# First layer's FFN shift and gate on VectorE, one unbroken norm-factor run, final products on two engines

## The chip, the cores and the metric

The kernel runs on one core of one Trainium2 chip. The metric is device time in microseconds (us) for one execution, as the median of several runs; lower is better. An execution holds a span, which the profile cuts into its engines' work, and a little time around it.

## The reference

Two layers of a diffusion backbone work on 384 token columns: 128 context tokens and 256 latent tokens. Each layer has six modulation vectors of 1024 channels, one column of each for the context tokens and one for the latent tokens. They come from one matrix product of a conditioning vector with `w_ada`:

```
mod = silu(c) @ w_ada[l] + b_ada[l]          # shift1, scale1, gate1, shift2, scale2, gate2
h = rms_norm(x) * (1 + scale1) + shift1
out = mix(h)                                  # three token mixers, gated, one output projection
x = x + gate1 * out
h = rms_norm(x) * (1 + scale2) + shift2
a, b = split(h @ w_ffn_in)
x = x + gate2 * ((silu(a) * b) @ w_ffn_out)
```

After both layers the output is `rms_norm(x, final_norm)`: x times one factor per token and one gain per channel.

## The kernel before

Activations are held transposed: 128 channels on the partitions, eight channel tiles, 384 tokens in the free direction. Every dense product is made in three matmuls of split operands: a weight piece of 128x1024 is loaded as `raw`, ScalarE rounds it to `wh`, and VectorE (for the FFN's second half every other time GpSimd) subtracts to get `wl` (`piece`, L659). One output tile of `dense_t` (L686) is 24 matmuls of 384 columns into a PSUM buffer `d`, of which there are three. `raw` has four buffers, `wh` and `wl` three each.

The weight pieces are read in one fixed order that `stream` (L64) writes down; the entries of other kinds that stand between them (`gate`, `ada`, `adv`) are worked off on the way by `piece`. All instructions are first recorded and then put in order by a planner (`Recorder.order`, L383): a list schedule with costs per instruction and an urgency per recorded operation, in which each engine takes the most urgent operation that is ready. Engines then run their instructions in that fixed order. One recorded operation is normally one instruction; one with several calls is never interleaved with others.

The parts around the change:

- **Modulation vectors of layer 0.** The first two are made at the start (`ada`, L753). The other four come in two groups of eight steps, spread over the 24 tiles of the first layer's branch projections. A step (`ada_step`, L791) loads two `raw` pieces and issues four fp32 matmuls of 512 columns on 32-column tiles (tile `m<-raw,silc`); after eight steps two ScalarE copies, four transposes (`m<-cst,sc`) and one addition of the bias follow. The places are ordered (L58-59), so that group 1 is gate1 and scale2, and group 2 is shift2 and gate2.
- **Modulation vectors of layer 1.** These are made on VectorE during the first layer's FFN (`ada_block`, L818): 48 blocks, each one `raw` piece and two VectorE instructions of 128x1024 that multiply it with one of two broadcast rows (tile `PL`) and sum it into one column of `mod`.
- **Norm factor.** `ssq` (L871) squares a channel tile on ScalarE and adds it into `nacc`; the eighth square isn't added. Matmuls with ones sum `nacc` and the eighth square over the partitions, three each (`m<-ones,nacc`, `m<-ones,sc`). `ssq_end` (L885) copies one result with ScalarE, adds the other, runs twelve small VectorE instructions on 128x3 (`rsqrt`, L739), makes three diagonal tiles and broadcasts them by one matmul. `norm_end` (L898) copies that to SBUF as `nacc` (named `rb` in the code). There are seven such norms: at the start, and in each layer after the SSD mixer, after the output projection and after the FFN. FFN tiles leave PSUM through a multiplication with `rb` (`sc<-d,nacc`), so the first of them waits for it.
- **Final norm.** Eight VectorE instructions multiply x by the gain and by the factor in PSUM (`PH<-PH,cst,m`), each followed by the DMA of its tile from SyncE.

## Time and profile before

| what | us |
|---|---|
| runs, median of 3 (lowest, highest) | 1911.48 (1909.68, 1913.89) |
| the profiled execution | 1913.74 |
| its span | 1912.0 |
| TensorE (PE) busy | 1864.8 |
| VectorE (DVE) busy | 1373.3 |
| ScalarE (ACT) busy | 944.3 |
| GpSimd (POOL) busy | 362.2 |

The profile's rows name an engine, an operation and the tiles it writes and reads. PE is the matmul part of TensorE, PEld its weight loads, which overlap the matmuls, and SPq the DMA queue of SyncE. Nearly all rows carry the line of the place that issues recorded operations (L516), so that the tile names tell them apart. A number in square brackets behind a row is the idle time of the engine before it, with what ended it.

### The profile page before, as it was taken

The page shows a single profiled execution, that of the slowest core. Times are in us where ns is not written, and L with a number is a line of the kernel's source. Part 1 is how long each engine was busy: PE and PEld are TensorE (multiplying, and loading weights), DVE is VectorE, ACT ScalarE, POOL GpSimd, SP SyncE. Part 2 cuts the span into 40 slices and gives each one's busy share as a digit, 9 for nine tenths or more (in the row PEclk, how much of TensorE's full clock was granted, in tenths as well). Part 3 has the DMA queues.
Part 4 walks back from the last instruction along what each step waited for, and adds up shares of the span by engine and source line. Part 5 has one row for each costly group of instructions (what it writes and reads, how often), then busy time and mean ns, then how long its engine had stood idle before and what let it go on. Part 6 is the DMA issues. An engine that isn't in the chain of part 4 may idle for free. (4 is left out here: it accounts for less than half of the span.)

```text
span 1912.0 us, 30336 instructions
## 1 busy us (share of the span) xinstructions
PE 1864.8 (98%) x10998; PEld 1726.6 (90%) x10998; DVE 1373.3 (72%) x2923; ACT 944.3 (49%) x1905; POOL 362.2 (19%) x362
## 2 busy tenths in 40 slices
PE   6999999999999999999999999999999999999997
PEld 5998998788988889999999889987879999999997
DVE  5847876888845598998978588768987567666522
ACT  4545555666522344443446556556755434444431
POOL 0112421230101111113511224112300022000132
PEclk9999999999999999999999999999999999999998
DMA  8566344664578766666654664346544554443341
GB/s 312 141 171 206 124 125 132 161 168 124 162 261 275 234 203 187 217 207 216 213 202 132 170 188 128 122 141 168 157 119 142 167 165 156 124 127 124 122 123 65
DMA packets 119318, 319.38 MB, mean 167 GB/s; under 512 B 13952, under 2 KB 57344, under 8 KB 117504
## 3 DMA queue, kind: packets, MB, share of 16 engines
q1 hardware_dynamic: 119168, 317.44, 54.3%
q8 instruction: 87, 1.43, 0.3%
q14 instruction: 63, 0.52, 0.1%
HBM read 296.59 MB, written 19.75 MB: 165 GB/s over the span
## 5 line engine op out<-in xcount | busy, mean ns | idle before, releaser
L516 ACT ACTIVATE wh<-raw 128x1024 fp32r<-128x1024 f32 x374 | 395.8, 1059 | 564.8 <-PE d L516 524.1
L516 DVE TENSOR_TENSOR wl<-raw,wh 128x1024 fp32r<-128x1024 f32 x352 | 454.9, 1293 | 226.3 <-ACT wh L516 223.6
L516 PE MATMUL d<-HH,wh 128*128 128x384 f32 x1448 | 496.5, 350 | 0.0
L516 PE MATMUL d<-HL,wh 128*128 128x384 f32 x1416 | 469.3, 337 | 0.0
L516 PE MATMUL d<-HH,wl 128*128 128x384 f32 x1384 | 466.5, 337 | 0.0
L516 PEld LDWEIGHTS d<-HH,wh 128*128 128x128 f32 x1448 | 273.1, 189 | 21.8 <-issue 15.9
L516 PEld LDWEIGHTS d<-HL,wh 128*128 128x128 f32 x1416 | 267.2, 189 | 0.6
L516 PEld LDWEIGHTS d<-HH,wl 128*128 128x128 f32 x1384 | 261.2, 189 | 0.0
L516 PE MATMUL d<-A,wh 128*128 128x386 f32 x744 | 255.4, 343 | 4.3 <-DVE sc L516 4.1
L516 PE MATMUL d<-C,wh 128*128 128x386 f32 x744 | 252.8, 340 | 0.0
L516 PE MATMUL d<-A,wl 128*128 128x386 f32 x744 | 252.8, 340 | 0.0
L516 PEld LDWEIGHTS d<-A,wh 128*128 128x128 f32 x744 | 140.9, 189 | 5.3 <-issue 4.4
L516 PEld LDWEIGHTS d<-C,wh 128*128 128x128 f32 x744 | 141.8, 191 | 0.4
L516 PEld LDWEIGHTS d<-A,wl 128*128 128x128 f32 x744 | 140.6, 189 | 0.0
L516 POOL TENSOR_TENSOR sc<-sc,sc 128x126 f32<-128x126 f32 x112 | 61.7, 569 | 272.4 <-DVE sc L516 159.7
L516 DVE SCALAR_TENSOR_TENSOR PH<-PL,n,cst 128x128 f32<-128x128 f32 x288 | 100.2, 381 | 14.6 <-PE l L516 5.3
L516 POOL TENSOR_TENSOR wl<-raw,wh 128x1024 fp32r<-128x1024 f32 x22 | 56.6, 2571 | 269.2 <-ACT sh L516 193.1
L516 PE MATMUL d<-wh,HH 128*128 128x512 f32 x240 | 98.1, 409 | 0.0
L516 PE MATMUL d<-wh,HL 128*128 128x512 f32 x240 | 95.0, 396 | 0.0
L516 PE MATMUL d<-wl,HH 128*128 128x512 f32 x240 | 95.0, 396 | 0.0
L516 PE MATMUL d<-PH,wh 128*128 128x384 f32 x256 | 87.2, 340 | 0.0
L516 PE MATMUL d<-PH,wl 128*128 128x384 f32 x256 | 86.1, 336 | 0.0
(260 smaller groups left out, 3130.3 us busy)
## 6 DMA issues: line engine op xcount, KB each, us to landing
raw<-in_ws SPq DMA_DIRECT2D x454, 512.0 KB, 3.7
PL<-rowr SPq DMA_DIRECT2D x48, 384.0 KB, 5.6
gd<-sc SPq DMA_DIRECT2D x48, 192.0 KB, 1.9
pb<-gd SPq DMA_DIRECT2D x48, 192.0 KB, 2.8
ex<-rowe SPq DMA_DIRECT2D x32, 128.0 KB, 3.7
ex<-rowe SPq DMA_DIRECT2D x16, 256.0 KB, 5.9
PH<-in_xT SPq DMA_DIRECT2D x2, 1536.0 KB, 7.4
yad<-pb SPq DMA_DIRECT2D x16, 192.0 KB, 1.9
```

Of the source, the lines that this page charges most:

```text
L516: tc.keep_in_program_order(getattr(engines[op.eng], meth)(*[real(a) for a in args], **{k: real(v) for k, v in kw.items()}))
```

## The change

- The eight steps of group 2 leave the stream. In their place 16 blocks of `ada_block`, for shift2 and gate2 of layer 0, stand around the eight steps of group 1. The broadcast rows for them lie in tile `F`. The number of weight pieces stays the same.
- The layer-1 blocks begin behind the fifth FFN piece of layer 0 instead of the first: 30 blocks now stand in 39 pieces of the first half and 18 in the second half, where 32 in 44 and 16 stood.
- `ssq` adds the eighth square too, on VectorE, and sums with three matmuls. `ssq_end` records the twelve small instructions, which now read PSUM directly, and the three diagonal tiles as one operation (`together`).
- In the last FFN ScalarE multiplies x by the final gain. At the end ScalarE copies the factor to SBUF, GpSimd multiplies tiles 0 and 1 by the copy, and VectorE the other six by the factor in PSUM.

```diff
+ADV_FROM = 5
...
-        s += main if l else main[:at] + spread(main[at:], steps(0, 1, 2))
+        late = []
+        for i, it in enumerate(steps(0, 1)):
+            late += [(("adv", 0, SHIFT2, i), 1), it, (("adv", 0, GATE2, i), 1)]
+        s += main if l else main[:at] + spread(main[at:], late)
...
-            at = len(blocks) * len(ff) // len(ff + fo)
-            s += spread(ff, blocks[:at]) + spread(fo, blocks[at:])
+            n = len(ff) - ADV_FROM
+            at = len(blocks) * n // (n + len(fo))
+            s += ff[:ADV_FROM] + spread(ff[ADV_FROM:], blocks[:at]) + spread(fo, blocks[at:])
...
+    @contextmanager
+    def together(self):
+        nc, calls = self.nc, []
+        class Collect:
+            def __getattr__(self, meth):
+                return lambda *a, **k: calls.append((meth, a, k))
+        old, nc.vector = nc.vector, Collect()
+        yield
+        nc.vector = old
+        op = self.rec.rec("vector", calls)
+        op.cost = max(op.cost, 0.196 * len(calls))
...
-        if self.spos == self.adv_at:
-            t = self.slot("PL", [P, 3, D])
+        if self.silb is None or self.silb[0] != l:
+            t = self.slot("PL" if l else "F", [P, 3, D])
...
-        elif j < KT - 1:
-            add(self.nacc, self.nacc, sq, ALU.add)
-        else:
+            return
+        (add if j < KT - 1 else self.tt)(self.nacc, self.nacc, sq, ALU.add)
+        if j == KT - 1:
             self.nps = self.mps()
-            for i, v in enumerate((self.nacc, sq)):
-                for t in range(3):
-                    self.mm(self.nps[:, 3 * i + t:3 * i + t + 1], v[:, t * P:t * P + P], self.ones[:, 0:1])
+            for t in range(3):
+                self.mm(self.nps[:, t:t + 1], self.nacc[:, t * P:t * P + P], self.ones[:, 0:1])
...
-        s = self.ring("r3", [P, 3])
-        self.act(s, self.nps[:, 0:3], AF.Copy)
-        self.tt(s, s, self.nps[:, 3:6], ALU.add)
-        self.rsqrt(r, s, 1.0 / n, eps, [P, 3])
         dg = self.sc()
-        for t in range(3):
-            self.ts(dg[:, t * P:t * P + P], self.ident, r[:, t:t + 1], ALU.mult)
+        with self.together():
+            self.rsqrt(r, self.nps[:, 0:3], 1.0 / n, eps, [P, 3])
+            for t in range(3):
+                self.ts(dg[:, t * P:t * P + P], self.ident, r[:, t:t + 1], ALU.mult)
...
                 if l + 1 < LAYERS:
                     self.scaled(l + 1, SHIFT1, SCALE1, j)
+                else:
+                    self.act(self.x[:, j], self.x[:, j], AF.Copy, scale=self.cst("fin")[:, j:j + 1])
...
-        for j in range(8):
-            self.stt(self.x[:, j], self.x[:, j], fin[:, j:j + 1], rb, ALU.mult, ALU.mult)
+        rs = self.sc()
+        self.act(rs, rb, AF.Copy)
+        for j in (0, 2, 3, 4, 5, 1, 6, 7):
+            if j < 2:
+                self.ptt(self.x[:, j], self.x[:, j], rs, ALU.mult)
+            else:
+                self.tt(self.x[:, j], self.x[:, j], rb, ALU.mult)
             self.dma(self.O["yT"][:, j], self.x[:, j])
```

How the order of instructions moves, at the three places that the prediction speaks of. Numbers behind a name tell buffers apart; PL with `mod_14` are the blocks of layer 1, F with `mod_13` those of layer 0, C the operand of the FFN, `rs` and `r` the norm factor.

VectorE at the step from the first layer's output projection to its FFN, before:

```order
L516 TENSOR_TENSOR r_1317_7330<-r_1317_7330,m_7318 128x3
L516 SCALAR_TENSOR_TENSOR C_7021<-PH_6953,mod_13_250,A_7013 128x128
L516 TENSOR_SCALAR rs_7342<-r_1317_7330 128x3
L516 SCALAR_TENSOR_TENSOR C_7021<-PH_6953,mod_13_250,A_7013 128x256
L516 TENSOR_SCALAR rs_7348<-rs_7342 128x3
L516 SCALAR_TENSOR_TENSOR PL_6956,mod_14_7104<-raw_7305,PL_6956 128x1024
L516 TENSOR_SCALAR rs_7348<-rs_7348 128x3
L516 SCALAR_TENSOR_TENSOR C_7021<-PH_6953,mod_13_250,A_7013 128x128
L516 SCALAR_TENSOR_TENSOR rs_7363<-rs_7348 128x3
L516 SCALAR_TENSOR_TENSOR raw_7305,mod_14_7104<-raw_7305,PL_6956 128x1024
```

The same place in the change:

```order
L523 TENSOR_TENSOR nacc_7002<-nacc_7002,sc_7269 128x384
L523 SCALAR_TENSOR_TENSOR PL_6939,mod_14_7284<-raw_7239,PL_6939 128x1024
L523 SCALAR_TENSOR_TENSOR C_7004<-PH_6936,mod_13_241,A_6996 128x128
L523 TENSOR_SCALAR rs_7294<-m_7286 128x3
L523 TENSOR_SCALAR rs_7296<-rs_7294 128x3
L523 TENSOR_SCALAR rs_7296<-rs_7296 128x3
L523 SCALAR_TENSOR_TENSOR rs_7299<-rs_7296 128x3
L523 TENSOR_TENSOR rs_7299<-rs_7299,rs_7294 128x3
```

The small instructions of the norm factor stood between blocks of layer 1 and now follow each other; one half of a block stands ahead of them.

VectorE in the first layer's branch projections, before:

```order
L516 SCALAR_TENSOR_TENSOR E_5996<-pb_5010,d_5990 128x384
L516 TENSOR_TENSOR wl_6053<-raw_5970,wh_6042 128x1024
L516 SCALAR_TENSOR_TENSOR E_5996<-pb_5033,d_6038 128x384
L516 TENSOR_TENSOR wl_6095<-raw_6011,wh_6084 128x1024
L516 SCALAR_TENSOR_TENSOR E_5996<-pb_5177,d_6080 128x384
```

The same place in the change:

```order
L523 SCALAR_TENSOR_TENSOR raw_5839,mod_13_241<-raw_5839,F_5306 128x1024
L523 SCALAR_TENSOR_TENSOR F_5306,mod_13_241<-raw_5862,F_5306 128x1024
L523 SCALAR_TENSOR_TENSOR C_2295<-sc_5893,C_2295 128x384
L523 SCALAR_TENSOR_TENSOR raw_5862,mod_13_241<-raw_5862,F_5306 128x1024
L523 TENSOR_TENSOR wl_5947<-raw_5843,wh_5925 128x1024
L523 TENSOR_TENSOR HL_5959<-C_2295,HH_5937 128x384 x3
L523 SCALAR_TENSOR_TENSOR E_5979<-pb_4832,d_5921 128x384
```

Between one weight tile `wl` and the next there now stand up to two blocks of two instructions each.

VectorE at the end of the program, before, with what an instruction waits for in brackets (PE_49, DVE_49 and Activation_49 are the counters of TensorE, VectorE and ScalarE):

```order
L516 SCALAR_TENSOR_TENSOR r_3372_19251<-rs_19242,rs_19239 128x3 [waits DVE_49]
L516 TENSOR_SCALAR sc_19253<-cst_97,r_3372_19251 128x128 [waits DVE_49]
L516 TENSOR_SCALAR sc_19253<-cst_97,r_3372_19251 128x128 x2
L516 SCALAR_TENSOR_TENSOR PH_16440<-PH_16440,cst_97,m_19257 128x384 [waits PE_49]
L516 SCALAR_TENSOR_TENSOR PH_16440<-PH_16440,cst_97,m_19257 128x384 x7
```

The same place in the change:

```order
L523 SCALAR_TENSOR_TENSOR r_3363_19217<-rs_19208,rs_19205 128x3 [waits DVE_49]
L523 TENSOR_SCALAR sc_19219<-cst_97,r_3363_19217 128x128 [waits DVE_49]
L523 TENSOR_SCALAR sc_19219<-cst_97,r_3363_19217 128x128 x2
L523 TENSOR_TENSOR PH_16408<-PH_16408,m_19223 128x384 [waits Activation_49]
L523 TENSOR_TENSOR PH_16408<-PH_16408,m_19223 128x384 x5
```

VectorE's first product waited for the broadcast matmul and now waits for ScalarE, whose last instruction is the copy of the same PSUM tile.

## Rows read from the trace of the kernel before

**Rows 1.** The page: busy time, share of the span and instructions of each engine.

```profile
PE 1864.8 (98%) x10998; PEld 1726.6 (90%) x10998; DVE 1373.3 (72%) x2923; ACT 944.3 (49%) x1905; POOL 362.2 (19%) x362
```

**Rows 2.** Stretches (us): length, busy time by engine, granted clock, DMA share, GB/s.

```profile
521.00:660.00 139.00, 137.44 (x792) 116.70 (x792) 70.38 (x92) 41.94 (x60) 19.20 (x21) 1.00 0.76 251
750.00:850.00 100.00, 100.00 (x566) 100.00 (x565) 94.98 (x153) 46.80 (x95) 16.53 (x12) 1.00 0.65 211
```

**Rows 3.** Timeline of PE around one step of the modulation matmuls: start, length, instruction.

```profile
521.18 0.34 PE L516 MATMUL d<-HL,wh 128*128 128x384 f32 x1
521.35 0.34 PE L516 MATMUL d<-HH,wl 128*128 128x384 f32 x1
521.62 1.07 PE L516 MATMUL m<-raw,silc 128*32 128x512 f32 x8
...
522.90 0.33 PE L516 MATMUL d<-HL,wh 128*128 128x384 f32 x1
```

**Rows 4.** Groups on PE, 521 to 660 us: busy, mean ns | idle before.

```profile
L516 PE MATMUL m<-raw,silc 128*32 128x512 f32 x128 | 20.7, 605 | 1.6 <-DMA raw<-in_ws 1.4
L516 PE MATMUL m<-cst,sc 128*128 128x128 f32 x8 | 1.3, 287 | 0.0
```

**Rows 5.** Waits, 521 to 660 us: total us, times, longest.

```profile
PEld m L516 <- DMA raw<-in_ws: 5.2, 6, 1.3
```

**Rows 6.** Timeline of PE: second half of one norm's sums, and the next matmul.

```profile
505.14 0.81 PE L516 MATMUL m<-ones,sc 128*128 128x1 f32 x6
505.81 0.42 PE L516 MATMUL d<-HH,wh 128*128 128x384 f32 x1
```

**Rows 7.** Timeline of PE at the first layer's step into its FFN.

```profile
708.71 0.34 PE L516 MATMUL d<-A,wl 128*128 128x386 f32 x1
713.17 0.41 PE L516 MATMUL d<-A,wh 128*128 128x386 f32 x1 [4.12 <-DVE sc L516]
...
717.81 0.34 PE L516 MATMUL d<-A,wl 128*128 128x386 f32 x1
```

**Rows 8.** The same place: timeline of DVE.

```profile
700.18 0.14 DVE L516 TENSOR_TENSOR r<-r,m 128x3 f32<-128x3 f32 x1
...
705.65 0.68 DVE L516 TENSOR_SCALAR sc<-cst,r 128x128 f32<-128x128 f32 x3
...
712.47 1.48 DVE L516 TENSOR_TENSOR sc<-d,nacc 128x384 f32<-128x384 f32 x3
```

**Rows 9.** The same place: ACT copies the factor out of PSUM.

```profile
708.09 0.49 ACT L516 ACTIVATE nacc<-m 128x384 f32<-128x384 f32 x1 [0.29 <-PE m L516]
```

**Rows 10.** The same place as a stretch, columns as in rows 2.

```profile
710.00:720.00 10.00, 6.83 (x30) 6.86 (x31) 9.27 (x17) 4.03 (x9) 1.38 (x1) 0.83 0.56 196
```

**Rows 11.** Groups on DVE, 750 to 850 us: the two instructions of a layer-1 block.

```profile
L516 DVE SCALAR_TENSOR_TENSOR PL<-raw,PL 128x1024 f32<-128x1024 f32 x18 | 24.7, 1375 | 0.4 <-DMA raw<-in_ws 0.4
L516 DVE SCALAR_TENSOR_TENSOR raw<-raw,PL 128x1024 f32<-128x1024 f32 x17 | 20.7, 1218 | 0.0
```

**Rows 12.** Tile wl on DVE, 539:580 and then 600:640 us: ns min/median/max.

```profile
L516 DVE TENSOR_TENSOR wl<-raw,wh x8: 1217/1226/1226, 540.0 to 575.5; 128x1024 fp32r<-128x1024 f32 x8
...
L516 DVE TENSOR_TENSOR wl<-raw,wh x8: 1809/1875/1885, 601.5 to 639.0; 128x1024 fp32r<-128x1024 f32 x8
```

**Rows 13.** Groups on DVE by form, whole span: the additions of squares.

```profile
L516 DVE TENSOR_TENSOR nacc<-nacc,sc 128x384 f32<-128x384 f32 x18 | 10.0, 556 | 10.1 <-ACT sc L516 9.4
```

**Rows 14.** Timeline of the end, all engines.

```profile
1899.68 0.17 ACT L516 ACTIVATE r<-m 128x3 f32<-128x3 f32 x1 [0.92 <-PE m L516]
...
1900.08 0.17 DVE L516 TENSOR_SCALAR rs<-r 128x3 f32<-128x3 f32 x1
...
1904.88 4.29 DVE L516 SCALAR_TENSOR_TENSOR PH<-PH,cst,m 128x384 f32<-128x384 f32 x8 [1.74 <-PE m L516]
1905.52 4.01 SPq L516 DMA_DIRECT2D out_yT<-PH  x8
```

**Rows 15.** One microsecond of the end as a stretch, columns as in rows 2.

```profile
1907.00:1908.00 1.00, 0.00 (x0) 0.00 (x0) 1.00 (x3) 0.00 (x0) 0.00 (x0) 0.50 1.01 366
```

More of the change, by code (lines that the diff above doesn't have):

```diff
@@ L818, in ada_block @@
     def ada_block(self, kind, l, place, j):
-        if self.spos == self.adv_at:
-            t = self.slot("PL", [P, 3, D])
+        if self.silb is None or self.silb[0] != l:
+            t = self.slot("PL" if l else "F", [P, 3, D])
             self.dma(t[:, 0:2], self.sild.rearrange("r p k -> r (p k)").unsqueeze(0).to_broadcast([P, 2, D]))
-            self.silb = t
+            self.silb = l, t
+        silb = self.silb[1]
         raw, = self.piece((kind, l, place, j), split=False)
@@ L826, in ada_block @@
             for r in range(2):
-                self.nc.vector.scalar_tensor_tensor(self.silb[:, 2] if r == 0 else raw, raw, 1.0, self.silb[:, r],
+                self.nc.vector.scalar_tensor_tensor(silb[:, 2] if r == 0 else raw, raw, 1.0, silb[:, r],
                                                     ALU.mult, ALU.mult, accum_out=self.mod_col(l, place, j, r))
@@ L865, in setup @@
             self.dma(self.sild.rearrange("r p k -> p r k"), rows)
-        self.adv_at = [k[0] for k, _ in self.stream].index("adv")
+        self.silb = None
         self.mod = [self.const(f"mod{i}", [P, 48, 2]) for i in range(2)]
@@ L1519, in run @@
         rb = self.ssq_end(EPS)
-        fin = self.cst("fin")
-        for j in range(8):
-            self.stt(self.x[:, j], self.x[:, j], fin[:, j:j + 1], rb, ALU.mult, ALU.mult)
+        rs = self.sc()
[5 more added lines that the diff above has]
+                self.tt(self.x[:, j], self.x[:, j], rb, ALU.mult)
             self.dma(self.O["yT"][:, j], self.x[:, j])
```

## Prediction

> **What bounds the kernel now.** I read the busy shares first. TensorE is busy 98% of the span, VectorE 72% [rows 1]. So an edit counts where it takes TensorE's time, fills one of its few gaps, or shortens the end of the program, where nothing else runs. Next I read the two stretches in which VectorE's load changes [rows 2]. In the first layer's branch projections TensorE is busy 137.4 of 139 us and VectorE 70.4. In the middle of the first layer's FFN VectorE is busy 95.0 of 100 us and TensorE all 100, so TensorE can stay full beside a VectorE that is nearly full. Then come single places: one modulation step [rows 3], the sums of one norm [rows 6], the step into the FFN [rows 7 to 10], the end [rows 14, 15].
>
> **Group 2 leaves TensorE.** Around a step, from the matmul at 521.35 to the second one behind it at 522.90, 1.55 us pass, where two ordinary intervals of 0.17 (521.18 to 521.35) would be 0.35 [rows 3]. One step costs 1.2 us, eight cost 9.6. The group's four transposes are half of 1.3 us [rows 4]; overlapped at the edges I take 0.5. Term: -10.1. Beside this TensorE's weight loads waited 5.2 us for raw pieces of these steps [rows 5]. Half of that could go too (-2.6). But the number of pieces is unchanged, so they must arrive in less time; I take nothing and keep -2.6 and +6 (as much again as now) as ends.
>
> **The 16 blocks on VectorE.** A block is 1.38 + 1.22 us [rows 11], 16 are 41.5 us. The branch stretch had 70.4 us of VectorE work [rows 2], so it gets 112 in about 139 - 10 = 129 us of TensorE: hidden on average. What hides it is the other 17 us. The first blocks stand where the third mixer's gates and the first branch operand are still being made, so the first weight tiles come late there; I charge one weight tile (1.22 us [rows 12]) and a little, +1.5, with ends 0 and +6 (four to five more weight tiles behind blocks). Two copies of the additions of the bias and the load of the broadcast rows go with this term.
>
> **Sums with three matmuls.** The second half of a norm's sums holds TensorE from 505.14 to 505.81, 0.67 us [rows 6]. It goes in seven places. At the start TensorE waits for loads anyway, and the last is on the closing chain (below): five count, -3.3. The added VectorE addition of 0.56 [rows 13] lies ahead of the sums, where TensorE has dense tiles to run. If it makes TensorE wait at each of the five, the term shrinks to -0.5; the other end is -3.3.
>
> **The step into the first layer's FFN.** All three PSUM buffers were full at 708.71 and TensorE stood still for 4.12 us until the first tile was multiplied by the norm factor [rows 7]. The factor took from 700.18 to 705.65 on VectorE because blocks of layer 1 stood between its small instructions, ScalarE's copy was ready at 708.58, and then blocks and weight tiles filled VectorE until 712.47 [rows 8, 9]. Behind the gap the granted clock averages 0.83 of full speed over 10 us [rows 10], which is the lower of its two levels for a part of it: the 17 intervals from 713.17 to 717.81 take 4.64 instead of 17 x 0.175 = 2.98 us, 1.66 more. Together 5.8 us. In the changed order the twelve small ones and the diagonals follow each other. At the end of the program, where nothing stands between them, they take from 1900.08 to 1904.88 - 1.74 = 1903.14 [rows 14], 3.1 us; I take that here. The first multiplication stands one half block and one operand piece behind them. One half block stands ahead of them, and TensorE has 21 matmuls (3.7 us) between the sums and the broadcast. Half block, piece and run are some 4.8 us from the end of the addition, the sums themselves take 0.7, so TensorE may wait up to 0.5 there. First multiplication some 10 us behind the last output tile, three tiles of TensorE work are 3 x 24 x 0.175 = 12.6: the gap closes. Term: -5.8 + 0.5 = -5.3; ends -5.8 and 0 (it is only moved).
>
> **Denser blocks in the FFN.** 30 in 39 pieces are 0.77 a piece, where 0.73 stood. With 24 pieces in 100 us that is one block more, 2.6 us [rows 11]: VectorE goes from 95.0 to 97.6 [rows 2]. Cost 0, hidden by the last 2.4 us; if they are gone, what is late next are weight tiles; end +4.
>
> **The end.** Between the eighth square and the factor one addition is put in, 0.56 + 0.05; ScalarE's copy and VectorE's addition, 0.40 from 1899.68 to 1900.08, go [rows 13, 14]: +0.2. Then, by the order above, VectorE's first product waits for ScalarE's copy of the factor, for which I take the same copy at 0.49 [rows 9], + 0.05: +0.55. In return six products are left on VectorE, of 0.54 each (4.29 / 8), and 1.1 us less. But behind the first product the DMA engines work at a share of 1.01, 366 GB/s [rows 15]: eight tiles of 0.197 MB need 4.3 us, just what the products took. The outputs are bound by the writing, so the split pays nothing. Term: +0.8; ends -0.3 (the 1.1 counts after all) and +1.3.
>
> **Sum.** -10.1 + 1.5 - 3.3 - 5.3 + 0 + 0.8 = -16.4. The profiled execution is 1913.7 (span 1912.0 and 1.7 around it) and gives 1897.3. It is 2.2 above the median of 1911.5, so on the median I predict 1895.
>
> **A rule against the change.** In [rows 12] a weight tile takes 1.23 us where GpSimd is idle and 1.88 where it adds up the branches, 0.65 more. The Trainium skill (SBUF — State Buffer, "Who interferes with whom") says that a VectorE instruction with two SBUF inputs and a GpSimd one that reads SBUF contend for a shared port, and that the loser blocks entirely; the trace agrees in direction, by 0.65 us. The new blocks have two SBUF inputs. That is the third rival.
>
> **The rivals.**
> 1. The loads hold the branch stretch. The DMA share there is 0.76 on average [rows 2] and raw pieces were already waited for [rows 5]. The same pieces in 129 us ask for 0.82. If the stretch can't become shorter, group 2 gives nothing: 1895 + 10 = 1905. Against it: 0.82 is under 1, and the blocks don't need TensorE's place to free a buffer. Chance 0.12.
> 2. The gap at the FFN stays, because the planner puts other work ahead of the multiplications than I count: 1895 + 5.3 = 1900. Against it: in the changed order only one whole block's worth stands between sums and multiplications. Chance 0.10.
> 3. The lock. GpSimd works 19.2 us in the branch stretch [rows 2]. If each of its instructions blocks VectorE for its whole length and none of this is yet in the 70.4, VectorE needs 112 + 19 = 131 us for 129: 2 to 4 more, 1898. Chance 0.08.
> 4. Slower than before: VectorE becomes the bound of the branch stretch. Every weight tile stands behind up to two blocks, in order. The point from which it decides is a mean of (129 - 70.4) / 32 = 1.8 us for one block instruction; from there each 0.1 us costs 32 x 0.1 = 3.2 us. At 2.4 us the gain is gone (1914), at 2.6 it is 1921. Against it: 1.22 to 1.38 us in a stretch with GpSimd at work [rows 11]. Chance 0.03.
> 5. The unbroken run isn't what costs: each small instruction still waits for the one before it through VectorE's own counter, as the order shows, so the run isn't faster by itself. Where TensorE has work enough (all norms but the step into the FFN) it saves nothing. That is in the sum already.
>
> **How the numbers follow.** My forecast has 0.67: 1895, by its own bounds 1888 to 1901. Rival 1 adds 1905 at 0.12. The range that leaves out 2 in 10 at most goes from 1888 (raw waits halved, FFN step without rest, other terms at their good ends) to 1904. A measurement of this kernel tells 0.2%, some 3.8 us, from no change, so faster means under 1907.7. The forecast, rivals 2 and 3 lie under it (0.85), rival 1 mostly (0.09 of 0.12). The rest: same 0.04, slower 0.02 with the worse half of rival 4. Faster 0.94.
>
> **What would show it.** Right: 64 records of `m<-raw,silc` in place of 128; VectorE at 110 to 118 us in the branch stretch beside a full TensorE; no idle time of over 1 us on TensorE and a granted clock of 1.00 at the step into the FFN; `m<-ones,sc` gone; a first product that waits for ScalarE, and a last product over 1 us earlier against the end of the writing than before. Wrong: TensorE idle for raw pieces or `wl` in the branch stretch by more than 5 us; a new gap where the factor is waited for, at the broadcast matmul or later in the FFN; an end that is shorter than 14.5 us from the last dense matmul.

## The result, and the profile after

The changed kernel takes 1892.09 us (median of 4 runs, 1890.23 to 1894.72) where the kernel before takes 1912.68 beside it: a ratio of 0.9896 with a 95% interval of 0.9884 to 0.9909, by which it is 19.9 us less. A second set of runs, below, gives 0.9881 (0.9864 to 0.9898). The forecast was 1895, in a range of 1888 to 1904. The profiled execution took 1894.72 with a span of 1892.9, against 1913.74 and 1912.0.

Busy shares of the change, from the page [rows 1]:

```profile
PE 1848.8 (98%) x10888; PEld 1718.8 (91%) x10888; DVE 1412.3 (75%) x2986; ACT 946.3 (50%) x1905; POOL 373.7 (20%) x364
```

The same two kinds of stretch as in [rows 2], in the change (length, busy time by engine, granted clock, DMA share, GB/s): the first layer's branch projections, then 100 us of its FFN.

```profile
519.00:649.00 130.00, 128.95 (x730) 115.97 (x729) 106.83 (x169) 43.22 (x62) 25.16 (x21) 1.00 0.83 269
730.00:830.00 100.00, 99.66 (x563) 99.36 (x562) 96.21 (x154) 45.35 (x91) 19.79 (x12) 1.00 0.71 218
```

TensorE stays full in both, and VectorE takes 106.8 of 130 us in the first, where it took 70.4 of 139. The groups on TensorE in that stretch [rows 4], and the waits of its weight loads there [rows 5]:

```profile
L523 PE MATMUL m<-raw,silc 128*32 128x512 f32 x64 | 13.1, 605 | 0.8 <-DMA raw<-in_ws 0.8
```

```profile
PEld m L523 <- DMA raw<-in_ws: 5.0, 6, 1.4
```

Half the matmuls are gone (64 of 128), and the waits for raw pieces are not: 5.0 us in place of 5.2.

The step into the first layer's FFN: TensorE's timeline around sums and broadcast [rows 7], then VectorE's [rows 8] and ScalarE's [rows 9].

```profile
682.92 0.34 PE L523 MATMUL d<-A,wh 128*128 128x386 f32 x1
...
686.10 0.72 PE L523 MATMUL m<-ones,nacc 128*128 128x1 f32 x6
...
690.26 0.34 PE L523 MATMUL d<-A,wl 128*128 128x386 f32 x1
690.44 0.81 PE L523 MATMUL m<-sc,ones 128*128 128x384 f32 x2
```

```profile
687.11 0.16 DVE L523 TENSOR_SCALAR rs<-m 128x3 f32<-128x3 f32 x1
...
689.47 0.68 DVE L523 TENSOR_SCALAR sc<-cst,r 128x128 f32<-128x128 f32 x3
...
692.95 1.02 DVE L523 TENSOR_TENSOR sc<-d,nacc 128x384 f32<-128x384 f32 x2 [1.27 <-PE d L523]
```

```profile
691.28 0.49 ACT L523 ACTIVATE nacc<-m 128x384 f32<-128x384 f32 x1 [6.12 <-PE m L523]
```

TensorE starts its first FFN matmul at 682.92. The broadcast matmul at 690.44 starts directly behind a dense one at 690.26, and the first tile is multiplied at 692.95, when VectorE waits for TensorE and not the other way round. The gap of 4.12 us is gone, and so is the lower clock behind it: the granted clock is 1.00 in each of the stretches from 685 to 730 us, against 0.83 in [rows 10].

The end, all engines [rows 14]:

```profile
1878.71 0.56 DVE L523 TENSOR_TENSOR nacc<-nacc,sc 128x384 f32<-128x384 f32 x1 [0.66 <-ACT sc L523]
...
1879.32 1.13 PE L523 MATMUL m<-ones,nacc 128*128 128x1 f32 x6 [2.05 <-DVE nacc L523]
...
1885.28 0.49 ACT L523 ACTIVATE sc<-m 128x384 f32<-128x384 f32 x1 [6.03 <-PE m L523]
1885.80 2.88 DVE L523 TENSOR_TENSOR PH<-PH,m 128x384 f32<-128x384 f32 x6 [2.26 <-ACT sc L523]
1885.85 1.96 POOL L523 TENSOR_TENSOR PH<-PH,sc 128x384 f32<-128x384 f32 x2 [16.68 <-ACT sc L523]
1886.38 3.81 SPq L523 DMA_DIRECT2D out_yT<-PH  x8
```

VectorE's first product waits for ScalarE's copy, as the order said. From there to the end of the span it takes 1892.94 - 1885.80 = 7.14 us, and before 1911.97 - 1904.88 = 7.09: two engines finish the products earlier, and the writing takes as long as ever. The three sums at 1879.32 take 1.13 us in this execution, at a granted clock of 0.66 on average, and 0.83 at the full clock in run 6 below.

**Where the time went.** Each profile holds the same 8996 dense matmuls (those that write a tile `d`), and none is missing. They stand in the same order but for at most 39 of them, all inside the pieces called start and FFN. So two kernels can be laid side by side by the start of the nth one, counted from 0. The table gives the time between such starts in us; columns: to the 2100th (start and first mixers), to the 2160th (sums of the norm behind the SSD mixer), to the 2880th (third mixer's rest and branch projections), to the 3240th (output projection's end and step into the FFN), to the 4560th (FFN), to the 4680th (norm), to the 6480th (second layer's mixers), to the 6600th (norm), from the 7380th to the 7500th (step into the second FFN), from the 8900th to the last, and from the last one's start to the end. The numbers ahead of the names are those of the runs below. The pieces left out, 6600 to 7380 and 7500 to 8900, are 135.20 and 246.43 in every profile.

```
                              start   sums  branch   step    FFN   sums  layer2   sums   sums   sums    end    span
before                      494.22  20.72 150.41  71.43 232.14  22.99 454.66  28.51  23.18  17.20  14.88  1912.0
 4 b1_late_blocks_alone     491.83  20.72 149.47  65.07 233.01  22.99 454.32  28.51  23.19  17.21  14.89  1902.8
the change                  493.75  19.74 141.00  64.42 232.68  22.30 454.78  27.73  22.44  16.47  16.01  1892.9
 6 r1_change_again          491.08  19.74 140.21  64.42 232.68  22.30 453.16  27.73  22.44  16.47  15.73  1887.6
 1 e1_group2_on_tensor      490.95  19.73 151.04  64.42 232.71  22.30 453.18  27.71  22.44  16.47  16.24  1898.8
 2 e2_norm_apart            492.29  20.30 140.35  64.39 232.23  22.29 452.98  27.88  22.40  16.47  15.71  1888.9
 3 e3_blocks_from_first     493.44  19.74 138.24  73.89 232.14  22.30 455.00  27.72  22.44  16.47  15.71  1898.7
 5 e4_two_sums              491.05  20.30 138.01  65.10 232.53  22.97 453.28  28.43  23.11  17.15  15.46  1889.0
 7 e5_no_copy_at_end        491.24  19.74 140.39  64.42 232.71  22.30 453.68  27.73  22.44  16.47  15.20  1887.9
 9 e6_all_on_vector         492.56  19.74 164.87  64.91 232.68  22.30 455.11  27.73  22.44  16.47  15.72  1916.1
 8 e8_steps_behind_tiles    490.44  19.74 149.53  64.42 232.89  22.30 452.58  27.73  22.44  16.47  15.74  1895.9
10 e9_branch_adds_on_vector 493.57  19.74 140.46  64.42 232.72  22.30 455.65  27.73  22.44  16.47  15.72  1892.8
11 e10_steps_later_no_copy  491.71  19.74 138.94  64.42 232.71  22.30 452.12  27.72  22.44  16.47  15.20  1885.4
12 e11_paying_parts         491.78  20.31 139.40  64.39 232.14  22.29 453.25  27.89  22.40  16.47  15.72  1887.7
```

In the change 9.4 us go in the branch stretch, 7.0 at the step into the FFN, and 0.98 + 0.69 + 0.78 + 0.74 + 0.73 = 3.9 in the five other pieces with sums; 1.1 come at the end and 0.5 in the FFN. The start and the second layer's mixers differ by 3 to 4 us between executions of nearly the same work, so a difference there in one profile says nothing of the change.

### The profile page after: what moved, and what is told of

Its sections match the earlier page's. It is cut to its first block, busy times and chain, and to the rows that moved or that the text cites. A ratio compares the mean times of both kernels' runs of the same rounds, so it can differ in the third digit from the quotient of the medians.

```text
span 1892.9 us, 30209 instructions
## 1 busy us (share of the span) xinstructions
PE 1848.8 (98%) x10888; PEld 1718.8 (91%) x10888; DVE 1412.3 (75%) x2986; ACT 946.3 (50%) x1905; POOL 373.7 (20%) x364
```

## The experiments

Theory: the gain is the sum of the forecast's terms, that is group 2 off TensorE with its blocks hidden, the step into the FFN, and the shorter sums, less the later end. Rivals: the loads hold the branch stretch; VectorE becomes its bound; one of the parts does nothing. The times below are medians and ratios to the kernel before on the same chip.

**1. Group 2 back on TensorE.** In the change:

```diff
-        late = []
-        for i, it in enumerate(steps(0, 1)):
-            late += [(("adv", 0, SHIFT2, i), 1), it, (("adv", 0, GATE2, i), 1)]
-        s += main if l else main[:at] + spread(main[at:], late)
+        s += main if l else main[:at] + spread(main[at:], steps(0, 1, 2))
```

> Undoes one part of the change: the eight steps of shift2 and gate2 stand on TensorE again, spread with group 1, and the 16 VectorE blocks are gone. By the forecast's sum the branch stretch gets 8 x 1.2 + 0.5 = 10.1 us longer, less what the blocks cost there (1.5 forecast; the aligned dense matmuls of the two profiles say 0.6): 8.6 to 9.5 us slower than the change, some 1901. By the rival that the loads hold the stretch, nothing is paid back: within 2 us of the change. If VectorE's blocks had made weight tiles late, the stretch would get shorter by it.

1901.61 us, ratio 0.9957 (0.9941 to 0.9974): 12 to 15 us slower than the change by the ratios of its two sets, 10.0 to 10.8 in the branch stretch (151.04 against 141.00 and 140.21), and nothing elsewhere that an execution doesn't vary by. So the blocks pay a little more than the sum said, and the loads do not hold the stretch.

**2. The factor's instructions separate again.**

```diff
-        with self.together():
-            self.rsqrt(r, self.nps[:, 0:3], 1.0 / n, eps, [P, 3])
-            for t in range(3):
-                self.ts(dg[:, t * P:t * P + P], self.ident, r[:, t:t + 1], ALU.mult)
+        self.rsqrt(r, self.nps[:, 0:3], 1.0 / n, eps, [P, 3])
+        for t in range(3):
+            self.ts(dg[:, t * P:t * P + P], self.ident, r[:, t:t + 1], ALU.mult)
```

> Undoes one part: the twelve small instructions and the three diagonal tiles are separate operations again, which the planner may interleave with blocks and weight tiles. If the unbroken run is what closed the step into the first layer's FFN, TensorE stands still there again for 2 to 4 us, with its lower clock behind it: 3 to 6 us slower than the change. If the later start of the layer-1 blocks or the dropped ScalarE copy closed it, there is no gap and the time is within 1 us of the change.

1889.08 us, ratio 0.9885 (0.9861 to 0.9909): the same as the change. The step takes 64.39 us, as with the run. VectorE's timeline there:

```profile
685.54 0.15 DVE L523 TENSOR_SCALAR rs<-m 128x3 f32<-128x3 f32 x1
685.62 1.22 DVE L523 SCALAR_TENSOR_TENSOR raw<-raw,PL 128x1024 f32<-128x1024 f32 x1
...
689.18 0.68 DVE L523 TENSOR_SCALAR sc<-cst,r 128x128 f32<-128x128 f32 x3
689.77 1.22 DVE L523 TENSOR_TENSOR wl<-raw,wh 128x1024 fp32r<-128x1024 f32 x1
...
694.33 1.01 DVE L523 TENSOR_TENSOR sc<-d,nacc 128x384 f32<-128x384 f32 x2
```

Half a block stands among the small instructions, and the chain from the first of them to the diagonals takes 689.18 - 685.54 = 3.6 us, where it takes 689.47 - 687.11 = 2.4 in the change. The difference of 1.2 us is the half block, and TensorE has tiles for it. The unbroken run isn't what closed the gap. In the table it is worth 0.56 us in the first piece with sums (19.74 against 20.30), and the FFN is 0.45 longer with it.

**3. The blocks of layer 1 from the first FFN piece again.**

```diff
-ADV_FROM = 5
+ADV_FROM = 0
```

> Undoes one part: the layer-1 blocks begin at the first FFN piece again (32 in 44 pieces). If the later start is what closed the step into the FFN, the gap of some 4 us comes back: 3 to 6 us slower than the change. If the unbroken run closed it, at most one whole block (2.6 us) more stands ahead of the first multiplication, for which TensorE has 12.6 us of tiles: no gap, within 1 us of the change.

1897.58 us, ratio 0.9933 (0.9914 to 0.9953): 7 to 10 us slower than the change by the ratios of its two sets, 9.5 at the step (73.89 against 64.42). The gap is back though the run is unbroken. TensorE's, ScalarE's and VectorE's timelines:

```profile
680.83 0.42 PE L523 MATMUL d<-A,wh 128*128 128x386 f32 x1 [0.82 <-ACT A L523]
...
689.95 0.72 PE L523 MATMUL m<-ones,nacc 128*128 128x1 f32 x6
...
701.52 0.66 PE L523 MATMUL d<-A,wh 128*128 128x386 f32 x1 [5.20 <-DVE sc L523]
```

```profile
694.76 0.49 ACT L523 ACTIVATE nacc<-m 128x384 f32<-128x384 f32 x1 [9.95 <-PE m L523]
695.17 2.95 ACT L523 ACTIVATE wh<-raw 128x1024 fp32r<-128x1024 f32 x3
```

```profile
683.41 2.04 DVE L523 SCALAR_TENSOR_TENSOR PL<-raw,PL 128x1024 f32<-128x1024 f32 x1
...
688.73 0.55 DVE L523 TENSOR_TENSOR nacc<-nacc,sc 128x384 f32<-128x384 f32 x1
...
693.08 0.68 DVE L523 TENSOR_SCALAR sc<-cst,r 128x128 f32<-128x128 f32 x3
...
696.26 3.50 DVE L523 TENSOR_TENSOR wl<-raw,wh 128x1024 fp32r<-128x1024 f32 x3 [0.70 <-ACT wh L523]
699.67 1.22 DVE L523 SCALAR_TENSOR_TENSOR raw<-raw,PL 128x1024 f32<-128x1024 f32 x1
...
700.82 1.48 DVE L523 TENSOR_TENSOR sc<-d,nacc 128x384 f32<-128x384 f32 x3
```

The factor's copy is in SBUF at 695.25, and the first tile is multiplied at 700.82. Between them stand three weight tiles, whose rounding ScalarE does only behind that copy, and half a block, 4.6 us from 696.26 on, while TensorE stands still with all `d` buffers full. That is one part of the delay. The other lies ahead of the norm: three block instructions (2.04, 1.21 and 1.21 us) stand on VectorE from 683.41 on, ahead of the eighth addition at 688.73, and the sums start 9.1 us behind TensorE's first FFN matmul, where the change has 3.2.

The way to the first multiplied tile can be laid out for the five orders. The table counts in us from the start of TensorE's first FFN matmul: to the start of the last sum, of the diagonals, to the end of the factor's copy, and to the start of the first multiplied tile. The last column counts VectorE's block instructions from 16 us ahead of that first matmul up to the first multiplied tile.

```
                          sums  diagonals    copy  multiplied  blocks
before                    5.49      11.55   14.48       18.38      11
 4 b1_late_blocks_alone   2.60       7.50    9.99       10.38       3
the change                3.65       6.55    8.85       10.03       2
 2 e2_norm_apart          3.65       7.82   10.63       12.97       4
 3 e3_blocks_from_first   9.59      12.25   14.42       19.98      11
```

In the change TensorE comes to its fourth FFN tile, which needs a free `d` buffer, at 14.0; the orders that multiply the first tile by 13.0 have no gap. Against the kernel before, the unbroken run does shorten the way from sums to diagonals, from 6.1 to 2.7 us. But there are as many blocks around the step. Nine of them now start ahead of the sums, where seven did, and the sums come 4.1 us later; behind the copy 5.6 us pass instead of 3.9. The run moves the blocks and does not take them away; the later start does.

**4. The later blocks alone, in the kernel before.**

```diff
+ADV_FROM = 5
...
-            at = len(blocks) * len(ff) // len(ff + fo)
-            s += spread(ff, blocks[:at]) + spread(fo, blocks[at:])
+            n = len(ff) - ADV_FROM
+            at = len(blocks) * n // (n + len(fo))
+            s += ff[:ADV_FROM] + spread(ff[ADV_FROM:], blocks[:at]) + spread(fo, blocks[at:])
```

> The kernel before, with one part of the change alone: the layer-1 blocks begin behind the fifth FFN piece. Theory after the first four runs: their place alone closes the step into the first layer's FFN, since weight pieces queue behind blocks there; then the 4.1 us of standstill and the 1.7 us of lower clock go, and 5 to 7 us with them: some 1905 beside 1911.5. Rival, that of the prediction: the small instructions of the factor stay interleaved and still hold the first multiplication: under 2 us gained.

1904.82 us, ratio 0.9965 (0.995 to 0.998), 6.7 us faster than the kernel before; the step takes 65.07 where it took 71.43. VectorE's timeline there:

```profile
694.58 0.15 DVE L519 TENSOR_TENSOR r<-r,m 128x3 f32<-128x3 f32 x1
...
694.98 1.22 DVE L519 SCALAR_TENSOR_TENSOR raw<-raw,PL 128x1024 f32<-128x1024 f32 x1
...
698.62 0.68 DVE L519 TENSOR_SCALAR sc<-cst,r 128x128 f32<-128x128 f32 x3
...
701.50 0.56 DVE L519 TENSOR_TENSOR sc<-d,nacc 128x384 f32<-128x384 f32 x1
```

The small instructions are still interleaved, ScalarE's copy and VectorE's addition are still there, and the gap is gone. Runs 2 to 4 together settle it: the place of the blocks alone closes the step, and the unbroken run is neither needed nor enough.

**5. Two sums again.** The eighth square gets matmuls of its own, and the copy and the addition return:

```diff
-        (add if j < KT - 1 else self.tt)(self.nacc, self.nacc, sq, ALU.add)
-        if j == KT - 1:
+        if j < KT - 1:
+            add(self.nacc, self.nacc, sq, ALU.add)
+        else:
             self.nps = self.mps()
-            for t in range(3):
-                self.mm(self.nps[:, t:t + 1], self.nacc[:, t * P:t * P + P], self.ones[:, 0:1])
+            for i, v in enumerate((self.nacc, sq)):
+                for t in range(3):
+                    self.mm(self.nps[:, 3 * i + t:3 * i + t + 1], v[:, t * P:t * P + P], self.ones[:, 0:1])
...
+        s = self.ring("r3", [P, 3])
+        self.act(s, self.nps[:, 0:3], AF.Copy)
         with self.together():
-            self.rsqrt(r, self.nps[:, 0:3], 1.0 / n, eps, [P, 3])
+            self.tt(s, s, self.nps[:, 3:6], ALU.add)
+            self.rsqrt(r, s, 1.0 / n, eps, [P, 3])
```

> Undoes one part: the eighth square is summed by three matmuls of its own again, ScalarE copies one result and VectorE adds the other at the start of the unbroken run. Forecast: 0.67 us of TensorE at each of five places, 3.3 us slower than the change; the end of the program 0.2 us shorter, and 0.7 us of TensorE's time behind the last dense tile's start moved. Rival: the added addition on VectorE is as late as the matmuls were long, then within 1 us of the change.

1892.16 us, ratio 0.9904 (0.9886 to 0.9923): the time alone can't tell it from the change. The table can: 0.56 + 0.68 + 0.67 + 0.70 + 0.67 + 0.68 = 4.0 us are back at six places (the second is in the step), and the end is 0.3 to 0.55 shorter. The branch stretch, whose code is the same, took 138.0 instead of 140.2 to 141.0 in the profiled execution and hides most of that there. It varies so by itself: in run 3 an order that is the change's, instruction by instruction, took 138.2.

**6. The change once more.** Nothing is edited.

> The changed kernel once more, unaltered, to see what differs between two executions of the same order. If the raw waits of the branch stretch (5.4 us in the first profile, 2.8 to 5.5 in the other kernels) are a matter of order, they are again 5.4 within 0.3; if of chance, they move by 1 to 3. The half clock behind the gap at 88 us (1.55 us in the first profile, absent in three of the four other kernels) is expected to come and go: the start is the same work in all of them. Time 1892, within 2.

1889.09 us (5 runs), ratio 0.9881. The raw waits moved from 5.0 us to 2.7, so they are partly chance, in the same order. The waits of TensorE's weight loads in this run's branch stretch:

```profile
PEld m L523 <- DMA raw<-in_ws: 2.7, 3, 1.5
```

And 1.54 us of the difference is TensorE's clock. Some 89 to 91 us after the start, in every kernel here, TensorE stands still for 1.38 to 1.40 us and then for 0.29 us. In the first profile of the change the clock falls behind it, in the second it doesn't. Two microseconds as stretches, of the first and of the second (columns as above; the clock stands ahead of the DMA share):

```profile
91.00:92.00 1.00, 1.00 (x5) 1.00 (x4) 0.00 (x0) 0.00 (x0) 0.71 (x2) 0.55 1.04 413
92.00:93.00 1.00, 1.00 (x5) 1.00 (x5) 0.00 (x0) 0.74 (x1) 0.00 (x0) 0.50 0.51 197
```

```profile
91.00:92.00 1.00, 1.00 (x8) 1.00 (x7) 0.00 (x0) 0.50 (x1) 0.40 (x1) 1.00 0.91 348
92.00:93.00 1.00, 1.00 (x7) 1.00 (x7) 0.40 (x1) 1.00 (x2) 0.00 (x0) 1.00 0.69 280
```

Half of full speed is the lower of the two levels, 1.2 of 2.4 GHz: five matmuls in a microsecond instead of eight. From the 540th to the 600th dense matmul it takes 14.7 us in three of the fourteen profiles and 13.1 in the others.

**7. The end without copy and GpSimd.**

```diff
-        rs = self.sc()
-        self.act(rs, rb, AF.Copy)
-        for j in (0, 2, 3, 4, 5, 1, 6, 7):
-            if j < 2:
-                self.ptt(self.x[:, j], self.x[:, j], rs, ALU.mult)
-            else:
-                self.tt(self.x[:, j], self.x[:, j], rb, ALU.mult)
+        for j in range(8):
+            self.tt(self.x[:, j], self.x[:, j], rb, ALU.mult)
```

> Changes the end alone: no ScalarE copy of the factor, no product on GpSimd; all eight products on VectorE, of the x that ScalarE has scaled, with the factor in PSUM. Forecast: the first product starts 0.55 us earlier behind the broadcast, the writing (7.1 us from the first product's start) stays: from the start of the last dense matmul to the end 15.5 us where the change has 16.0; 0.5 us faster, under what the times can tell. Rival: the products bound the end and the split paid: 1.1 us later at the last product, then 0.5 us slower.

1888.76 us, ratio 0.9877 (0.9859 to 0.9895). From the last dense matmul to the end 15.20 us, against 15.73 and 16.01 in the two profiles of the change. VectorE's products in the timeline:

```profile
1880.78 3.81 DVE L523 TENSOR_TENSOR PH<-PH,m 128x384 f32<-128x384 f32 x8 [1.74 <-PE m L523]
```

The first starts when TensorE's broadcast is done, 8.05 us behind the last dense matmul where it starts at 8.57 with the copy ahead of it and the full clock (run 6), and the end follows 1887.93 - 1880.78 = 7.15 us later, as with six products. The split saves nothing, and the wait for its copy costs 0.5 us.

**8. The remaining steps later.** The matmuls of `ada_step` get the urgency of dense ones:

```diff
-        self.rec.rec("tensor", [("matmul", (ps[32 * j:32 * j + 32], self.silc[:, k, :], raws[j // 2][:, j % 2 * 512:j % 2 * 512 + 512]),
-                                 dict(start=k == 0, stop=k == KT - 1, tile_position=(0, 32 * j))) for j in range(4)])
+        with self.urgency(DENSE):
+            self.rec.rec("tensor", [("matmul", (ps[32 * j:32 * j + 32], self.silc[:, k, :], raws[j // 2][:, j % 2 * 512:j % 2 * 512 + 512]),
+                                     dict(start=k == 0, stop=k == KT - 1, tile_position=(0, 32 * j))) for j in range(4)])
```

> The change, with the eight steps of group 1 placed behind the weight tiles that precede them in the program (the urgency of dense matmuls), some 50 matmuls later on TensorE than now. If the planner puts each step ahead of the landing of its raw pieces, the raw waits (5.4 us in the profile of the change) go to under 1: 3 to 5 us faster. Rival: two of the four raw buffers stay held for some 9 us longer at each step, the next weight pieces are loaded later, and TensorE waits for weight tiles instead: 0 to 8 us slower.

1901.73 us, ratio 0.9944 (0.9925 to 0.9964): 9 to 12 us slower than the change by the ratios. No step waits for raw pieces any more, and the branch stretch takes 149.53 us. TensorE's waits in it, of the matmuls and of the weight loads:

```profile
PE d L523 <- DVE wl L523: 7.4, 7, 2.6
```

```profile
PEld d L523 <- DVE wl L523: 10.3, 9, 2.9
```

The rival holds: the waits for raw pieces are the cheap side of a trade. A step that waits for nothing holds two of four buffers longer, and what waits for raw pieces then is the rounding of weight pieces on ScalarE, 64.6 us in this run against 21.2 in the change:

```profile
ACT wh L523 <- DMA raw<-in_ws: 64.6, 18, 6.5
...
ACT wh L523 <- DMA raw<-in_ws: 21.2, 6, 6.0
```

The weight tiles come late behind it. In the smaller dose of run 11, 9 matmuls later, the stretch took 138.9 us and the time didn't change.

**9. All four vectors on VectorE.**

```diff
-        for i, it in enumerate(steps(0, 1)):
-            late += [(("adv", 0, SHIFT2, i), 1), it, (("adv", 0, GATE2, i), 1)]
+        for i in range(KT):
+            late += [(("adv", 0, g, i), 1) for g in (GATE1, SCALE2, SHIFT2, GATE2)]
```

> The change with group 1 (gate1, scale2) on VectorE too: 32 blocks stand in the branch projections and no step is left. The branch stretch lasts 140 to 141 us in the change (520 dense matmuls apart from start to start), with 105 us of VectorE work in 128 of it. Forecast from the fourth rival: TensorE would need 140 - 15 = 125 us, VectorE 105 + 16 x 2.44 = 144 and more, so VectorE is the bound, weight tiles are late, and the stretch takes 144 to 152 us: 4 to 12 us slower than the change. Rival, that VectorE is hidden on average as long as blocks can be put off: 127 us, 13 us faster.

1915.0 us, ratio 1.0025 (1.001 to 1.0039). The fourth rival is real, with a higher price than expected: the branch stretch takes 164.9 us. The stretch from 519 us, and TensorE's longest waits to 684 us:

```profile
519.00:649.00 130.00, 106.75 (x568) 104.03 (x567) 120.07 (x195) 35.43 (x51) 19.64 (x17) 0.88 0.72 230
```

```profile
PE m L523 <- DVE xn L523: 8.7, 2, 8.1
...
PE d L523 <- ACT PH L523: 8.1, 1, 8.1
```

VectorE is busy 120 of 130 us, and two waits of 8.1 us each, which end at 548 and 598 us, are for the first branch operand and the third mixer's last steps; both stand behind blocks on VectorE. The granted clock averages 0.88 in this stretch. With 16 blocks VectorE had 23 us to spare in 130; 16 more of 2 x 1.22 us are 39.

**10. The branch additions on VectorE.**

```diff
-                        self.ptt(acc[:, j], acc[:, j], th, ALU.add)
+                        (self.ptt if l else self.tt)(acc[:, j], acc[:, j], th, ALU.add)
```

> The change with the first layer's branch additions (15 of 128x384 in the stretch) on VectorE instead of GpSimd. If the two engines hold each other up, weight tiles that took 1.9 to 2.0 us beside GpSimd take 1.23 again, VectorE gets 15 x 0.55 = 8.3 us of additions and loses some 13 x 0.65 = 8: no change of its load, and the time within 2 us of the change, since the stretch is bound by TensorE. If the lock is what leaves TensorE waiting for raw pieces and weight tiles there, 2 to 4 us faster.

1891.13 us, ratio 0.9913 (0.9896 to 0.9929): no faster than the change, and the branch stretch is 140.5 us. VectorE's weight tiles (ns, least, median and most) in this run, and in the change:

```profile
L523 DVE TENSOR_TENSOR wl<-raw,wh x28: 1217/1219/1382, 518.5 to 646.0; 128x1024 fp32r<-128x1024 f32 x28
```

```profile
L523 DVE TENSOR_TENSOR wl<-raw,wh x28: 1214/1225/2034, 519.4 to 646.6; 128x1024 fp32r<-128x1024 f32 x28
```

The engines do hold each other up, and it costs no time here, since VectorE had 23 us to spare in 130.

**11. Steps a little later, with the end of run 7.** The end as in 7, and in `ada_step` the same edit as in 8 with less delay:

```diff
+        with self.urgency(DENSE - 30):
```

> The end without copy and GpSimd products, and the steps of group 1 moved back by 9 dense matmuls (1.6 us) in the middle of the eight, between the change and the run with 50. If a little later is late enough for the raw pieces and early enough for the buffers, the raw waits (3.7 to 5.4 us in the change) fall to under 2 and no weight tile is late: 2 to 3 us faster than the change, some 1887. Rival: each wait that goes from the steps comes back at weight tiles, twice over as in the run with 50 (4 us gone, 9 to 10 us lost): no change or 2 to 4 us slower.

1889.75 us, ratio 0.9903 (0.9888 to 0.9918). The steps with their waits took 12.7 us (15.0 and 13.3 in the profiles of the change), which is within what an unaltered order varies by. Nothing gained.

**12. Only the parts that pay.** The edits of runs 2 and 7 together.

> The change without the two parts that the runs so far show no gain for: the factor's instructions are separate operations again, and the end is eight VectorE products with the factor in PSUM, without copy and GpSimd. Kept are the blocks of shift2 and gate2 on VectorE, the three sums, and the later start of the layer-1 blocks. Theory: these three carry the gain; from the last dense matmul to the end 15.2 us beside 15.7 to 16.0, the step into the FFN 64.4 us (360 dense matmuls) as in the change: ratio 0.988, 0.5 us faster than the change, which the times can't tell. Rival, that the unbroken run has a part in it somewhere: 1 to 3 us slower than the change.

1888.84 us (5 runs), ratio 0.9886 (0.987 to 0.9902): the gain of the change without its run and its split. It can't be told faster than the change. The end took 15.72 us and not 15.2, because its three sums ran at the lower clock (1.36 us, against 0.83 in run 7).

## Why the prediction was right, point by point

It forecast 16.4 us less; the ratios say 19.9 and, on the second set, 22.7. In the first profile the terms below add up to -18.7, where the span is 19.1 shorter. The second profile is 5.3 us shorter still, in pieces that vary by chance: 2.7 at the start (1.5 of it the clock), 0.8 in the branch stretch, 1.6 in the second layer's mixers and 0.3 at the end. The good ends that the prediction names add up to 1889.4, not to the 1888 at which its range begins.

- **Group 2 (-10.1).** Right. The time that steps add, summed over the records, was 24.5 us for sixteen and 15.0 for eight in the change (13.3 in its second profile), of which 1.2 x 16 and 1.2 x 8 are the steps themselves; four transposes took 0.5. So 9.6 + 0.5 is confirmed, and run 1 gives it back. That the raw waits would neither grow nor go was right in the first profile (5.0 against 5.2) and by chance 2.3 better in the second. Runs 3, 6 and 7 have the order of the change in this stretch and took 138.24, 140.21 and 140.39 us, where it took 141.00: a reading of the stretch is sure to about 3 us.
- **The 16 blocks (+1.5).** The stretch lost 9.4 us and the steps and transposes 10.0, so the blocks cost 0.6; in the second profile 1.4, and by the same reckoning nothing in runs 3 and 7, where the steps add 12.7 and 14.8. So this term is not confirmed beyond "small". The prediction put it where the third mixer's last steps stand behind blocks; run 9, with twice the blocks, shows two waits of 8.1 us for such work.
- **Sums (-3.3).** Right mechanism, undersized: run 5 gives 4.0 back at six places, 0.56 to 0.70 at each. The step that failed is "five count": the closing norm's first three matmuls stood ahead of the last dense tile and held TensorE there too (17.20 against 16.47). The six places gained 4.6, because in the first of them the unbroken run is worth some 0.5 us more (run 2); the fifth rival had it save nothing there.
- **The step into the FFN (-5.3).** The size was near, 7.0 less the 0.7 of the sums there, and that is luck, since the cause was wrong. The prediction charged the factor's way on VectorE, "because blocks of layer 1 stood between its small instructions", and let the run close the gap. Runs 2 and 4 leave the small instructions apart, with half a block in between, and have no gap; run 3 has the run and a gap. What closes it is the edit that the prediction treated as "Denser blocks in the FFN" and put at nothing. Its reading of the kernel before holds: blocks stood in the chain, and "blocks and weight tiles filled VectorE until 712.47". What failed is the step from there to the run: with 11 block instructions around the step, closing the chain moves them ahead of the sums and the weight tiles behind the copy (run 3). With five FFN pieces free of blocks only 2 to 4 are left there. The 0.5 us kept for a wait at the broadcast did not come: it runs directly behind a dense matmul.
- **Denser blocks (0).** The FFN took 0.5 us more, and not by the density alone: with the same blocks and the run taken apart it took 232.23 us (run 2), 0.1 more than before. In 215 us with VectorE at 95% busy, TensorE waited once for a multiplied tile:

```profile
820.77 0.42 PE L523 MATMUL d<-A,wh 128*128 128x386 f32 x1 [0.34 <-DVE sc L523]
```

- **The end (+0.8).** 1.1 and 0.85 in the two profiles, of which the lower clock of the sums is 0.3 in the first: the wait for the copy is there, the writing sets the end, and the split pays nothing (run 7).
- **The signs.** All signs of being right came except one: VectorE was to be busy for 110 to 118 us in the branch stretch and is for 106.8 of 130. The 32 block instructions take 1.22 us each there, 39 us, and not the 41.5 of [rows 11]. The limit of 5 us for TensorE's waits in that stretch could not tell right from wrong: its loads waited 5.0 for raw pieces, and 5.2 before.
- **The rivals.** Loads holding the stretch: refuted by run 1. The gap that stays: it would have, without the later blocks. The lock: no time (run 10). VectorE as the bound: not at 16 blocks, at 32 (run 9).

On the lock, the Trainium skill (SBUF — State Buffer, "Who interferes with whom") has the engine that issues first keep the shared port and the other block entirely. The runs agree that GpSimd is the other party: without its additions the longest weight tile falls from 2.03 to 1.38 us. They agree on the order too: five of the additions in the change met a block, each began 0.16 to 0.23 us behind it and took 1.87 to 1.93 us, and the block kept its 1.22. The additions in the change, beside a median of 1.02 us before:

```profile
L523 POOL TENSOR_TENSOR E<-E,pb x15: 992/1256/1997, 584.1 to 646.4; 128x384 f32<-128x384 f32 x15
```

## What to carry to other kernels

When an engine that is the bound stands still at a step, look at what its releaser does in order ahead of the release, tile by tile, and also ahead of the norm that it waits for; here the number of blocks around the step counted, and closing the chain of small instructions, which one sees first, only moved them. Undo each part of a change alone and do the suspected part alone: the later start of the blocks carried a third of the gain, and two parts carried none that can be told. Where times vary by more than an edit is worth, count the same matmuls in two profiles and compare stretch by stretch.

## What the runs showed of the hardware

- The same instructions with the same standstill (1.4 and 0.29 us, some 90 us after the start) are followed by the full clock in eleven profiles and by half of it in three, for 1.55 us of loss. A sum of terms can't know such a term; one profile can be off by it in either direction.
- Which of two instructions that meet is lengthened goes, with few exceptions, by which began first. In the change's branch stretch all 32 block instructions take 1.21 to 1.23 us; the five that met a GpSimd addition had begun ahead of it. In the first layer's FFN 19 of the 96 begin while an instruction of GpSimd is running, and 16 of these take over 1.3 us, up to 3.47; none of the other 77 does. The two rows are the 96:

```profile
L523 DVE SCALAR_TENSOR_TENSOR PL<-raw,PL x48: 1209/1221/3365, 685.7 to 947.3; 128x1024 f32<-128x1024 f32 x48
L523 DVE SCALAR_TENSOR_TENSOR raw<-raw,PL x48: 1209/1218/3472, 690.1 to 948.6; 128x1024 f32<-128x1024 f32 x48
```
